# A hybrid attention and DeltaNet layer on one core: the modulation sums of the first stage regrouped, and the attention join moved from VectorE to ScalarE

## The chip, the cores and the metric

The kernel runs on one core of one Trainium2 chip. The core has TensorE (PE in the rows; PEld is its weight load), VectorE (DVE), ScalarE (ACT), GpSimd (POOL) and SyncE (SP), which here only issues loads and stores. The metric is the device time of one launch in microseconds. All tensors are float32; products use fp32r parts.

## The reference

One layer: a modulation vector from the conditioning vector, a wide projection, windowed attention beside a gated DeltaNet, an output projection, and an MLP. What the change touches is the start and the end of the attention:

```
mod = silu(c) @ w_ada + b_ada                 # (1024) @ (1024, 6144)
sh1, sc1, gt1, sh2, sc2, gt2 = split(mod, 6)
u = x * (1.0 + sc1) + sh1                     # (1024, 1024)
proj = u @ w_in                               # q, k, v, DeltaNet inputs, gates
...
o = einsum(probs, v)                          # 16 heads of 64, window of 128
```

## The kernel before

The first stage makes `u`, feature-major, in eight blocks of 128 features. For block `k`, TensorE transposes eight tiles of `x` (`u_turn`, step `t`) into one PSUM bank `b` and one bank `a`; ScalarE reads each bank twice with scale `sc1[:, k]` and bias `sh1[:, k]` (`u_out`, step `o`), once rounded to fp32r (`uh`) and once exact (`utm`); VectorE subtracts the two into the low part `ul`. Then 12 products of 512 columns use the block (`u_mm`, step `m`): two heads of DeltaNet keys, two halves, three products for the split operands.

Before that the block's 128 shifts and 128 scales must exist. Each is a dot product of `silu(c)` with a column of `w_ada`, 8 partial products of 128 rows. They are split by engine: for blocks 2 to 7 the shift is summed by GpSimd (`ada_pool`: a product over 128x1024 and three adds), the scale by VectorE for rows 0 to 5 (`ada_acc`, step `v`: one TENSOR_SCALAR and five SCALAR_TENSOR_TENSOR of 128 columns) and by TensorE for rows 6 and 7 (products of one column with `c_col`, step `p`). TensorE sums the 128 partitions of each partial result with a product against `ones` (step `s`), and VectorE adds the bias into `sc1` and `sh1` (`ada_end`). In block 0 VectorE sums the shift and TensorE the scale; in block 1 GpSimd the shift and TensorE the scale.

The order in which TensorE, VectorE and ScalarE get this work is written by hand, as a string of steps, and the three engines run it in that order. SyncE issues the loads in one queue (`a0 x a1 x d a2 x a3 x ...`: `a` is a block of `w_ada`, two loads of 512 KB; `x` a block of x, 512 KB; `d` two blocks of `w_in`). A load waits when its buffer is still in use: GpSimd, VectorE and TensorE all hold buffers of `w_ada`.

After the first stage come the value projection and the key heads (`pa`), then the attention: 64 items of two heads by 128 queries, threaded between 26 units of 48 products that make queries, keys and gates. Every 16 products one item is started; `after(n, f)` records `f` n products later. The item's last step is `att_values`: four products of 256 columns into the only buffer of PSUM tag `c`. Its two halves of 64 partitions hold two partial sums that must be added. `top` copies the lower half to SBUF (`bot`, ScalarE, five products later) and `join` adds it to the upper half, read from PSUM, in two VectorE operations of 64x128 (four products after that). The bank `c` is free for the next item when the second of these ends. VectorE has long operations in its queue at that time: the triangular solve (`stt`, `M`), weight splits (`wl`), and query splits (`qs`). GpSimd adds the two window halves of the probabilities there (`sm`) and masks them (`pl`).

Of the kernel before, what the change touches and what calls it, by code (L numbers as in the profile page):

```python
# [17 lines left out]
P = 128  # L18
# [16 lines left out]
def hybrid_layer_kernel(ctx: ExitStack, tc: tile.TileContext,  # L35
# [261 lines left out]
    BLK = [(j * P, P) for j in range(KT)]  # L297
    adav, adaa, adat = {}, {}, {}

    ALL = range(KT)  # L300
# [11 lines left out]
    def ada_load(blk):  # L312
        lo, n = BLK[blk]
        m = 2 if n == 256 else 1
        kk = KT // m
        for i in range(m):
            for sec in (0, 1):
                t = ada_tile([P, kk, n])
                nc.sync.dma_start(out=t, in_=w_ada[i * kk * P:(i + 1) * kk * P, sec * D + lo:sec * D + lo + n]
                                  .rearrange("(k p) c -> p k c", p=P))  # L320
                adat[sec, blk, i] = t
                adav.setdefault((sec, blk), []).extend(t[:, k, :] for k in range(kk))

    def ada_acc(sec, blk, ks=range(KT)):
        n = BLK[blk][1]
        if ks[0] == 0:
            adaa[sec, blk, V] = p0.tile([P, n], F32, tag="adaacc1" if sec else "adaaccv", name="adaacc", bufs=1 + sec)
        acc = adaa[sec, blk, V]
        for k in ks:
            w = adav[sec, blk][k]  # L330
            if k == 0:
                V.tensor_scalar(out=acc, in0=w, scalar1=c_col[:, 0:1], scalar2=None, op0=ALU.mult)
            else:
                V.scalar_tensor_tensor(out=acc, in0=w, scalar=c_col[:, k:k + 1], in1=acc, op0=ALU.mult, op1=ALU.add)

    def ada_pool(sec, blk):

# [10 lines left out]
    adap = {}

    def ada_sums(blk, direct):  # L350

        m = BLK[blk][1] // P
        if blk not in adap:
            adap[blk] = psum("a", 2)
        t = adap[blk]
        for sec in (0, 1):
            for j in range(m):
                js = slice(j * P, (j + 1) * P)
                for i, (E, ks) in enumerate(ada_on[sec, blk]):
                    o = 4 * i + 2 * sec + j  # L360
                    if E is T and direct:
                        for k in ks:
                            T.matmul(t[:, o:o + 1], lhsT=adav[sec, blk][k][:, js], rhs=c_col[:, k:k + 1],
                                     start=k == ks[0], stop=k == ks[-1])
                    elif E is not T and not direct:
                        T.matmul(t[:, o:o + 1], lhsT=adaa[sec, blk, E][:, js], rhs=ones[:, 0:1], start=True, stop=True)

    def ada_end(blk):
        lo, n = BLK[blk]
        j0, m = lo // P, n // P  # L370
        t = adap[blk]
        if len(ada_on[1, blk]) > 1:
            V.tensor_tensor(out=sc1[:, j0:j0 + m], in0=t[:, 6:6 + m], in1=bada[:, KT + j0:KT + j0 + m], op=ALU.add)
        V.scalar_tensor_tensor(out=sc1[:, j0:j0 + m], in0=t[:, 2:2 + m], scalar=1.0,
                               in1=sc1[:, j0:j0 + m] if len(ada_on[1, blk]) > 1 else bada[:, KT + j0:KT + j0 + m],
                               op0=ALU.add, op1=ALU.add)
        sh = sh1[:, j0:j0 + m]
        V.tensor_tensor(out=sh, in0=t[:, 0:m], in1=bada[:, j0:j0 + m], op=ALU.add)
        if len(ada_on[0, blk]) > 1:
            V.tensor_tensor(out=sh, in0=t[:, 4:4 + m], in1=sh, op=ALU.add)  # L380
# [11 lines left out]
    rows_a = p0.tile([P, 2 * P], F32, tag="adaacc1", name="rows_a", bufs=2)[:, 0:P]  # L392
# [31 lines left out]
    def u_mm(k):  # L424
        for half in range(2):
            for i in range(2):
                wh, wl = wdk[i]
                for m in range(3):
                    w, xx = ((wh, uh), (wh, ul), (wl, uh))[m]
                    T.matmul(raw_acc[i][half], lhsT=w[:, k, :], rhs=xx[k][:, halves[half]], start=k == 0 and m == 0,  # L430
                             stop=k == KT - 1 and m == 2)

# [1574 lines left out]
```

## Time and profile before

| | |
|---|---|
| Time, median of 3 runs | 1866.16 us (1865.82 to 1868.0) |
| Time of the profiled execution | 1864.97 us |
| Its span, first to last instruction | 1863.3 us |
| TensorE busy | 1820.0 us (98%) |
| VectorE, ScalarE, GpSimd busy | 1306.0, 976.9, 338.5 us |
| Mean granted TensorE clock, of full speed | 0.993 |

The profiled execution has 1.7 us around its span. TensorE is busy for all but 43 us of it, so what shortens the kernel is work taken from TensorE, or one of the stretches in which it waits or runs at the lower clock.

### The profile page before, as it was taken

Reading aid. Unit: us, or ns where it says so; the run is one execution under the profiler, and the core shown is the slowest. Engines: PE = TensorE matmul, PEld = TensorE weight load, DVE = VectorE, ACT = ScalarE, POOL = GpSimd, SP = SyncE. Lnnn points to the kernel's source line nnn. Section 1 sums busy time; section 2 is a strip of 40 time slices with the busy share of each in tenths; the row PEclk is TensorE's granted clock in tenths of the full one; section 3 lists DMA queues with packets and bytes.
Section 4 is the critical chain, followed back from the end, with each engine's and each line's share of the span. In section 5 each row is a group of like instructions: output and inputs, shape, how many; then the busy total and the mean of one; then the engine's idle time right before and its main releaser. Section 6 shows DMA issues by size and latency. Waiting matters only on the chain.

```text
span 1863.3 us, 26105 instructions
## 1 busy us (share of the span) xinstructions
PE 1820.0 (98%) x9161; PEld 1503.1 (81%) x9161; DVE 1306.0 (70%) x2473; ACT 976.9 (52%) x2105; POOL 338.5 (18%) x493
## 2 busy tenths in 40 slices
PE   7999999999999999999999999999999999999997
PEld 5977878878788788888878888877788888888886
DVE  7677688898875566666553445788867776576697
ACT  3789656666664454455553323466555555434441
POOL 7323323443332000000001100002212120000000
PEclk8999999999999999999999999999999999999999
DMA  9655642232248444554355644358887879755671
GB/s 260 178 181 199 216 106 73 84 98 71 69 161 245 131 134 134 160 149 147 111 161 179 212 147 157 116 163 306 301 294 258 264 248 392 279 187 181 196 256 46
DMA packets 262414, 337.74 MB, mean 181 GB/s; under 512 B 26005, under 2 KB 171110, under 8 KB 262026
## 3 DMA queue, kind: packets, MB, share of 16 engines
q1 hardware_dynamic: 222954, 212.94, 36.5%
q0 software_dynamic: 31328, 108.44, 17.3%
q10 hardware_dynamic: 8000, 14.68, 2.2%
q8 instruction: 72, 1.18, 0.3%
q14 instruction: 60, 0.49, 0.1%
HBM read 231.40 MB, written 102.51 MB: 179 GB/s over the span
## 4 chain that ended last, share of the span: by engine, by line
PE 77%; DVE 9%; ACT 4%; DMA 3%; issue 2%; POOL 0%; ACTq 0%; SPq 0%; POOLq 0%; DVEq 0%
PE mm L248 32%; PE mm L1870 7%; PE mm L1930 6%; PE b L1930 4%; PE a L1930 4%; PE b L1870 3%; PE a L1870 2%; PE mm L1499 2%; PE c L1930 2%; PE c L909 2%; PE a L1499 1%; DVE wl L216 1%; PE mm L188 1%; PE mm L187 1%; PE mm L186 1%
## 5 line engine op out<-in xcount | busy, mean ns | idle before, releaser
L248 PE MATMUL mm<-uh,wl 128*128 128x512 f32 x800 | 331.3, 414 | 0.0
L248 PE MATMUL mm<-ul,wh 128*128 128x512 f32 x800 | 320.8, 401 | 0.0
L248 PE MATMUL mm<-uh,wh 128*128 128x512 f32 x800 | 317.3, 397 | 0.0
L216 DVE TENSOR_TENSOR sp<-sraw,sp 128x1024 fp32r<-128x1024 f32 x112 | 132.8, 1219 | 76.8 <-ACT sp L215 76.8
L215 ACT ACTIVATE sp<-sraw 128x1024 fp32r<-128x1024 f32 x112 | 112.7, 1053 | 122.5 <-PE b L1930 75.4
L248 PEld LDWEIGHTS mm<-ul,wh 128*128 128x128 f32 x800 | 150.5, 188 | 26.6 <-issue 0.2
L248 PEld LDWEIGHTS mm<-uh,wl 128*128 128x128 f32 x800 | 151.2, 189 | 22.9 <-issue 3.9
L248 PEld LDWEIGHTS mm<-uh,wh 128*128 128x128 f32 x800 | 151.2, 189 | 21.3 <-issue 0.2
L1930 PE MATMUL mm<-sp 128*128 128x512 f32 x528 | 136.9, 390 | 0.6 <-DVE sp L216 0.6
L1930 PEld LDWEIGHTS mm<-sp 128*128 128x128 f32 x528 | 98.5, 188 | 21.5 <-DVE sp L216 1.4
L216 DVE TENSOR_TENSOR wl<-wr,wh 128x1024 fp32r<-128x1024 f32 x81 | 98.6, 1218 | 8.0 <-ACT wh L215 8.0
L215 ACT ACTIVATE wh<-wr 128x1024 fp32r<-128x1024 f32 x81 | 85.1, 1050 | 22.1 <-PE c L1499 13.8
L1930 PE MATMUL a<-sp 128*128 128x512 f32 x336 | 92.6, 389 | 0.0
L1169 ACT ACTIVATE vn<-a,brk 128x128 f32<-128x128 f32 x64 | 23.5, 368 | 108.1 <-PE a L1167 107.1
L1930 PE MATMUL b<-sp 128*128 128x512 f32 (+1 forms) x336 | 80.0, 374 | 0.0
L842 DVE CUSTOM_DVE_ANT_0 nscore<-a,amask,nsink 128x256 f32<-128x256 f32 (+1 forms) x128 | 54.6, 464 | 33.4 <-PE a L835 32.6
L1930 PEld LDWEIGHTS a<-sp 128*128 128x128 f32 x336 | 63.1, 188 | 13.1
L853 POOL TENSOR_TENSOR sm<-sm 128x256 f32<-128x256 f32 x56 | 55.7, 995 | 97.6 <-ACT sm L849 65.0
L1930 PEld LDWEIGHTS b<-sp 128*128 128x128 f32 x336 | 60.5, 188 | 11.2
L216 DVE TENSOR_TENSOR wl<-fraw,wh 128x1024 fp32r<-128x1024 f32 x43 | 52.5, 1222 | 21.9 <-ACT wh L215 21.5
L849 ACT ACTIVATE sm<-nscore,stat 128x257 f32<-128x257 f32 (+1 forms) x128 | 62.1, 488 | 5.3 <-DVE stat L842 4.9
L215 ACT ACTIVATE wh<-fraw 128x1024 fp32r<-128x1024 f32 x43 | 45.0, 1055 | 33.2 <-PE b L1870 16.3
(524 smaller groups left out, 4669.7 us busy)
## 6 DMA issues: line engine op xcount, KB each, us to landing
wr<-in_w_in_dram SPq DMA_DIRECT2D x60, 512.0 KB, 3.6
sraw<-hf_d SPq DMA_DIRECT2D x54, 512.0 KB, 4.4
fraw<-in_w_ff_dram SPq DMA_DIRECT2D x32, 512.0 KB, 5.2
sraw<-wt_d SPq DMA_DIRECT2D x32, 512.0 KB, 4.3
hf_d<-t ACTq DMA_DIRECT2D x48, 256.0 KB, 4.1
wt_d<-wx POOLq DMA_DIRECT2D x48, 256.0 KB, 3.0
sraw<-in_w_ff_dram SPq DMA_DIRECT2D x22, 512.0 KB, 5.4
adaw<-in_w_ada_dram SPq DMA_DIRECT2D x41, 256.0 KB, 2.7
```

The source lines that it names most:

```text
L186: T.matmul(t, lhsT=wh[:, k, :], rhs=xh[k][:, sl], start=k == 0, stop=False)
L215: A.activation(out=hi, in_=src, func=AF.Copy)
L216: after(lag, lambda: V.tensor_tensor(out=lo, in0=src, in1=hi.bitcast(F32), op=ALU.subtract))
L248: T.matmul(ts[half], lhsT=w[:, k, :], rhs=xx[k][:, sl], start=k == 0 and m == 0, stop=k == KT - 1 and m == 2)
L842: V.tensor_tensor_reduce(out=ns[:, i, 1:1 + W], in0=sc[:, i * 2 * P:i * 2 * P + W], in1=amask[:, mo:mo + W], scale=-1.0, scalar=nsink[:, 2 ...
L849: A.activation(out=sm[:, i, 0:1 + W], in_=ns[:, i, 0:1 + W], func=AF.Exp, scale=-1.0, bias=st[:, i:i + 1], accum_out=st[:, 2 + i:3 + i])
L853: G.tensor_tensor(out=sm[:, :, 1 + P:1 + 2 * P], in0=sm[:, :, 1:1 + P], in1=sm[:, :, 1 + P:1 + 2 * P], op=ALU.add)
L909: T.matmul(av[:, 0:256], lhsT=vt[:, b, :], rhs=p_[:, m, :], start=p_ is full and m == 0, stop=p_ is prods[-1][1] and m == 1)
L1169: after(1, lambda: A.activation(out=vn, in_=Wp[:, 0:P], func=AF.Copy, scale=brk[:, n, h:h + 1]))
L1499: T.matmul(pt, lhsT=m[k][:, tok], rhs=w[:, k % 2, :], start=k == 0 and w is wh and m is mh, stop=k == KT - 1 and m is ml)
L1870: T.matmul(pt, lhsT=a[:, k0 + k, :], rhs=b[k], start=begin and k == 0 and x_ == 0, stop=k == 3 and x_ == 2, skip_group_check=True)
L1930: T.matmul(to, lhsT=a[:, f, t * P:(t + 1) * P], rhs=b[:, f, lo:up], start=(begin or own) and s % NS == 0 and f == 0 and x_ == 0, stop=s % ...
```

## The change

Four edits. Block `k` of `w_ada` now lies in tiles with shift and scale side by side, four row groups to a tile (each tile two loads of 256 KB, 32 loads instead of 16). GpSimd has no part in the sums. VectorE sums shift and scale of a block in one chain of operations 256 columns wide: five of the eight row groups in block 0, four in block 1, seven in blocks 2 to 7 (`ADV`); TensorE takes the rest as one-column products that accumulate into the same PSUM columns as the sum over partitions. The step string is new: TensorE's one-column products of block k+1 stand inside block k-1's products (`mid`), and VectorE's chain of block k+1 is spread around block k's steps. Four small constant operations (`trim`, `sel`) move from later code, where they were scheduled automatically, into the string (`c0`). In the attention, ScalarE copies all four 64x128 quarters of the result out of PSUM, and VectorE adds two SBUF tiles in one operation of 128x128.

```diff
-    ada_on = {(0, 0): [(V, ALL)], (1, 0): [(T, ALL)], (0, 1): [(G, ALL)], (1, 1): [(T, ALL)]}
-    for b in range(2, KT):
-        ada_on[0, b], ada_on[1, b] = [(G, ALL)], [(V, range(6)), (T, range(6, 8))]
+    ADV = [5, 4] + [7] * (KT - 2)
+    w_ada2 = w_ada[:, 0:2 * D].rearrange("(k p) (s d) -> p s k d", p=P, s=2)
...
+        for i in range(2):
+            t = ada_tile([P, 2, 4, P])
             for sec in (0, 1):
+                nc.sync.dma_start(out=t[:, sec, :, :], in_=w_ada2[:, sec, 4 * i:4 * i + 4, blk * P:(blk + 1) * P])
...
-    def ada_pool(sec, blk):
...
+    def ada_direct(blk):
+        adap[blk] = t = psum("a", 2)
+        for sec in (0, 1):
+            for k in range(ADV[blk], KT):
+                T.matmul(t[:, sec:sec + 1], lhsT=adav[blk][k][:, sec, :], rhs=c_col[:, k:k + 1],
+                         start=k == ADV[blk] and sec == 0, stop=False)
+    def ada_sums(blk):
+        for sec in (0, 1):
+            T.matmul(adap[blk][:, sec:sec + 1], lhsT=adaa[blk][:, sec, :], rhs=ones[:, 0:1], start=False, stop=sec == 1)
...
-    def u_mm(k):
+    def u_mm(k, mid=None):
         for half in range(2):
             for i in range(2):
+                if mid and (half, i) == (0, 1):
+                    mid()
...
-    for step in ('t0 s0 o00 o01 w0 w1 d4 t1 s1 v203 o10 v235 o11 v256 m0 t2 p2 s2 v304 o20 v346 o21 m1 t3 p3 s3 v404 o30 v446 o31 m2 '
+    steps = 'p0 v05 b0 t0 s0 v12 e0 o00 o01 w0 v14 w1 p1 d4 t1 s1 v22 e1 v24 o10 v26 o11 v27 m02 t2'
+    for k in range(2, 7):
+        steps += f' s{k} v{k + 1}2 e{k} v{k + 1}4 o{k}0 v{k + 1}6 o{k}1 v{k + 1}7 m{k - 1}{k + 1} t{k + 1}'
+    steps = steps.replace('o50', 'r0 o50').replace('t7', 't7 s7 e7 o70 o71 c0 m6')
...
-        def top():
-            A.activation(out=bot, in_=av[64:128, 0:256], func=AF.Copy)
-            after(4, join)
+        def copy():
+            for i in range(2):
+                for k, dst in ((1, bot), (0, o[:, sl])):
+                    A.activation(out=dst[64 * i:64 * i + 64, :], in_=av[64 * k:64 * k + 64, i * P:(i + 1) * P], func=AF.Copy)
+            after(5, join)
 
         def join():
-                V.tensor_tensor(out=o[64 * i:64 * i + 64, (n % 2) * P:(n % 2 + 1) * P],
-                                in0=av[0:64, i * P:(i + 1) * P], in1=bot[:, i * P:(i + 1) * P], op=ALU.add)
+            V.tensor_tensor(out=o[:, sl], in0=o[:, sl], in1=bot, op=ALU.add)
...
-        after(5, top)
+        after(5, copy)
```

VectorE's queue around block 2's scale and shift, before. `adaacc` is a partial sum, `ul1` the low part of block 1, `a_395` the PSUM columns of block 2's sums:

```order
L332 TENSOR_SCALAR adaacc_358<-adaw_185,c_col_113 128x128
L334 SCALAR_TENSOR_TENSOR adaacc_358<-adaw_185,c_col_113,adaacc_358 128x128 x2
L422 TENSOR_TENSOR ul1_131<-utm_362,uh1_123 128x512
L334 SCALAR_TENSOR_TENSOR adaacc_358<-adaw_185,c_col_113,adaacc_358 128x128 x2
L422 TENSOR_TENSOR ul1_131<-utm_368,uh1_123 128x512
L334 SCALAR_TENSOR_TENSOR adaacc_358<-adaw_185,c_col_113,adaacc_358 128x128
L373 TENSOR_TENSOR sc1_121<-a_395,cols_116 128x1
L374 SCALAR_TENSOR_TENSOR sc1_121<-a_395,sc1_121 128x1
L378 TENSOR_TENSOR sh1_120<-a_395,cols_116 128x1
```

The same engine and place in the changed kernel; `a_363` are block 2's columns, `adaacc_342` block 2's chain and `adaacc_387` block 3's:

```order
L380 TENSOR_TENSOR ul1_131<-utm_355,uh1_123 128x512
L324 SCALAR_TENSOR_TENSOR adaacc_342<-adaw_190,c_col_113,adaacc_342 128x256
L322 TENSOR_SCALAR adaacc_387<-adaw_195,c_col_113 128x256
L324 SCALAR_TENSOR_TENSOR adaacc_387<-adaw_195,c_col_113,adaacc_387 128x256
L342 TENSOR_TENSOR sc1_121<-a_363,cols_116 128x1
L342 TENSOR_TENSOR sh1_120<-a_363,cols_116 128x1
L324 SCALAR_TENSOR_TENSOR adaacc_387<-adaw_195,c_col_113,adaacc_387 128x256 x2
L380 TENSOR_TENSOR ul2_132<-utm_394,uh2_124 128x512
L324 SCALAR_TENSOR_TENSOR adaacc_387<-adaw_198,c_col_113,adaacc_387 128x256
L324 SCALAR_TENSOR_TENSOR adaacc_387<-adaw_198,c_col_113,adaacc_387 128x256
L380 TENSOR_TENSOR ul2_132<-utm_400,uh2_124 128x512
L324 SCALAR_TENSOR_TENSOR adaacc_387<-adaw_198,c_col_113,adaacc_387 128x256
```

Two operations of the next block's chain now stand ahead of a block's `sc1` and `sh1`, and the rest of it between the two `ul`.

TensorE's queue in block 1's products before (`uh1`, `ul1` are the block, `a_440` the columns of block 3):

```order
L413 MATMUL a_386<-ident_89,xin_187 128x128 x4
L363 MATMUL a_395<-c_col_113,adaw_185 128x1 x2
L366 MATMUL a_395<-ones_94,adaacc_236 128x1
L366 MATMUL a_395<-ones_94,adaacc_358 128x1
L430 MATMUL mm_263<-uh1_123,wh_179 128x512
L430 MATMUL mm_263<-ul1_131,wh_179 128x512
L430 MATMUL mm_263<-uh1_123,wl_180 128x512
L430 MATMUL mm_265<-uh1_123,wh_181 128x512
```

And now, where `a_408` are the columns of block 3:

```order
L371 MATMUL a_376<-ident_89,xin_193 128x128 x4
L337 MATMUL a_363<-ones_94,adaacc_342 128x1 x2
L390 MATMUL mm_235<-uh1_123,wh_183 128x512
L390 MATMUL mm_235<-ul1_131,wh_183 128x512
L390 MATMUL mm_235<-uh1_123,wl_184 128x512
L331 MATMUL a_408<-c_col_113,adaw_198 128x1 x2
L390 MATMUL mm_237<-uh1_123,wh_185 128x512
```

The one-column products of block 3 have moved from behind the transposes of block 3 to the fourth place of block 1's products, so TensorE meets them about one block earlier.

ScalarE's queue at one attention item before, `c_2542` being the bank of the values:

```order
L883 ACTIVATE ph_2534<-b_2531 128x256
L914 ACTIVATE bot_2545<-c_2542 64x256
L861 ACTIVATE sm_2495<-sm_2495,stat_2496 128x128 x2
L849 ACTIVATE sm_2550,stat_2551<-nscore0_2090,stat_2551 128x257 x2
L215 ACTIVATE wh_2578<-wr_2387 128x1024
```

And now, `c_2526` being that bank:

```order
L853 ACTIVATE ph_2518<-b_2515 128x256
L890 ACTIVATE bot_2530<-c_2526 64x128
L890 ACTIVATE at_2529<-c_2526 64x128
L890 ACTIVATE bot_2530<-c_2526 64x128
L890 ACTIVATE at_2529<-c_2526 64x128
L831 ACTIVATE sm_2479<-sm_2479,stat_2480 128x128 x2
```

Three more operations stand ahead of the scaling of a later item's probabilities (`sm`), and no VectorE operation reads the bank any more.

## Rows read from the trace of the kernel before

**Rows 1.** Busy time of each engine by stretch (us from the span's start; then the stretch's length, busy us and number of instructions of each engine, granted TensorE clock as a share of full speed, DMA share, GB/s); four stretches of the first stage and one of the attention.

```profile
10.00:20.00 10.00, 9.76 (x53) 8.05 (x54) 6.98 (x12) 4.68 (x6) 5.07 (x5) 0.67 1.12 323
20.00:30.00 10.00, 5.96 (x27) 4.85 (x27) 9.42 (x11) 2.79 (x4) 9.61 (x7) 0.84 1.18 319
30.00:40.00 10.00, 9.18 (x41) 7.42 (x42) 9.23 (x15) 3.36 (x5) 9.42 (x8) 0.84 1.08 287
40.00:50.00 10.00, 5.75 (x26) 4.65 (x25) 9.42 (x17) 4.62 (x8) 6.72 (x7) 0.67 0.66 173
...
300.00:350.00 50.00, 48.20 (x256) 40.30 (x255) 43.18 (x105) 32.98 (x95) 21.41 (x25) 1.00 0.25 81
```

**Rows 2.** What TensorE waited for over the whole span: the instruction that waited, who released it, us in total, times, longest.

```profile
PE a L366 <- DVE adaacc L334: 7.5, 3, 3.5
PE c L909 <- DVE at L922: 6.4, 10, 1.5
```

**Rows 3.** TensorE in order of time in the first stage (start us, us, engine, line, operation, tiles; in brackets the idle time before it and who ended it). L430 is a product of a block, L366 the sum over partitions, L532 the first product of the value projection.

```profile
34.31 0.39 PE L430 MATMUL c<-uh,wl 128*128 128x512 f32 x1
...
36.99 0.48 PE L430 MATMUL mm<-uh,wh 128*128 128x512 f32 x1
...
46.45 0.59 PE L366 MATMUL a<-ones,adaacc 128*128 128x1 f32 x2 [3.36 <-DVE adaacc L334]
...
47.48 0.63 PE L430 MATMUL mm<-ul,wh 128*128 128x512 f32 x1
...
53.00 0.48 PE L430 MATMUL mm<-uh,wh 128*128 128x512 f32 x1
...
57.68 0.48 PE L430 MATMUL mm<-uh,wh 128*128 128x512 f32 x1
...
67.96 0.50 PE L532 MATMUL b<-wvh,uh 128*128 128x272 f32 x2
```

**Rows 4.** VectorE in order of time in the first stage. L334 is the chain of partial sums, L373 and L374 the first operation on a block's scale, L422 a block's low part, L126 the low part of weights.

```profile
18.60 2.36 DVE L126 TENSOR_TENSOR wl<-wr,wh 128x1024 fp32r<-128x1024 f32 x2 [0.18 <-ACT wh L125]
20.88 0.15 DVE L374 SCALAR_TENSOR_TENSOR sc<-a,cols 128x1 f32<-128x1 f32 x1
...
31.21 3.63 DVE L334 SCALAR_TENSOR_TENSOR adaacc<-adaw,c_col,adaacc 128x128 f32<-128x128 f32 x3
...
47.27 0.16 DVE L374 SCALAR_TENSOR_TENSOR sc<-a,sc 128x1 f32<-128x1 f32 x1
...
47.73 1.12 DVE L334 SCALAR_TENSOR_TENSOR adaacc<-adaw,c_col,adaacc 128x128 f32<-128x128 f32 x3
49.07 0.69 DVE L422 TENSOR_TENSOR ul<-utm,uh 128x512 fp32r<-128x512 f32 x1 [0.22 <-ACT utm L421]
49.68 0.73 DVE L334 SCALAR_TENSOR_TENSOR adaacc<-adaw,c_col,adaacc 128x128 f32<-128x128 f32 x2
...
62.38 0.16 DVE L373 TENSOR_TENSOR sc<-a,cols 128x1 f32<-128x1 f32 x1 [0.45 <-PE a L366]
...
66.86 2.36 DVE L126 TENSOR_TENSOR wvl<-wr,wvh 128x1024 fp32r<-128x1024 f32 x2 [0.24 <-ACT wvh L125]
```

**Rows 5.** GpSimd in order of time in the first stage: the product of a block's shift, and the last add of a later block's.

```profile
31.27 2.05 POOL L341 TENSOR_TENSOR adaw<-adaw,c_col 128x1024 f32<-128x1024 f32 x1 [0.19 <-DVE adaacc L332]
...
46.33 0.98 POOL L346 TENSOR_TENSOR adaacc<-adaw 128x128 f32<-128x128 f32 x1
```

**Rows 6.** ScalarE in order of time in the first stage: the rounding of the two key weights, and a block's first exact pass.

```profile
17.50 2.01 ACT L125 ACTIVATE wh<-wr 128x1024 fp32r<-128x1024 f32 x2
...
48.27 0.77 ACT L421 ACTIVATE utm<-b,sh,sc 128x512 f32<-128x512 f32 x1
```

**Rows 7.** Groups of VectorE instructions by shape, whole span (line, operation, tiles, shapes, count, busy us, mean ns of one, idle before).

```profile
L1025 DVE SCALAR_TENSOR_TENSOR ada<-adaw,c_col,ada 128x512 f32<-128x512 f32 x39 | 29.1, 745 | 2.9 <-DMA adaw<-in_w_ada_dram 2.9
...
L1131 DVE SCALAR_TENSOR_TENSOR E<-b,rk,E 128x128 f32<-128x128 f32 x64 | 19.0, 345 | 10.3 <-PE b L1127 10.3
...
L602 DVE CAST gT<-zer 64x1024 fp32r<-64x1024 f32 x1 | 0.8, 764 | 0.1
```

**Rows 8.** Groups by shape in the attention (240 to 580 us), of ScalarE, VectorE and GpSimd: the copy out of PSUM, the join, a product over two SBUF tiles, and the add of the window halves.

```profile
L914 ACT ACTIVATE bot<-c 64x256 f32<-64x256 f32 x64 | 24.5, 382 | 5.4 <-issue 2.7 <-PE c L909 1.3
...
L922 DVE TENSOR_TENSOR at<-c,bot 64x128 f32<-64x128 f32 x128 | 35.6, 278 | 6.6 <-ACT bot L914 5.7
...
L732 DVE TENSOR_TENSOR stt<-M 128x122 f32<-128x122 f32 x1 | 0.3, 286 | 0.0
...
L853 POOL TENSOR_TENSOR sm<-sm 128x256 f32<-128x256 f32 x56 | 55.7, 995 | 97.6 <-ACT sm L849 65.0 <-issue 28.0 <-PE b L877 4.3
```

**Rows 9.** Two places of the attention in order of time, of three engines: L861 scales an item's probabilities, L877 transposes them on TensorE, L909 are the products with the values, L914 and L922 copy and join.

```profile
296.61 0.70 ACT L861 ACTIVATE sm<-sm,stat 128x128 f32<-128x128 f32 x2 [1.82 <-DVE stat L856]
...
335.10 0.38 ACT L914 ACTIVATE bot<-c 64x256 f32<-64x256 f32 x1
335.38 0.69 ACT L861 ACTIVATE sm<-sm,stat 128x128 f32<-128x128 f32 x2
...
336.92 0.38 PE L877 MATMUL b<-ident,sm 128*128 128x128 f32 x2
...
338.53 0.57 DVE L922 TENSOR_TENSOR at<-c,bot 64x128 f32<-64x128 f32 x2
...
339.24 0.47 PE L909 MATMUL c<-ph,vhl 128*128 128x256 f32 x2 [1.47 <-DVE at L922]
```

More of the change, by code (lines that the diff above doesn't have):

```diff
@@ L294, in dummies @@
             T.matmul(warm, lhsT=wz[:, 0:P], rhs=wz, start=True, stop=True)
[L297 to L303 removed]
+    ADV = [5, 4] + [7] * (KT - 2)
+    adav, adaa, adap = {}, {}, {}
+    w_ada2 = w_ada[:, 0:2 * D].rearrange("(k p) (s d) -> p s k d", p=P, s=2)
     aslot = ["gate", "gate", "ks", "wh", "wl", "wh", "wl"] + ["gate", "gate", "ks", "adaw", "adaw"] * 4
@@ L312, in ada_load, with ada_acc @@
     def ada_load(blk):
[L313 to L316, printed above, removed]
+        for i in range(2):
+            t = ada_tile([P, 2, 4, P])
             for sec in (0, 1):
[L318 to L325, printed above, removed]
+                nc.sync.dma_start(out=t[:, sec, :, :], in_=w_ada2[:, sec, 4 * i:4 * i + 4, blk * P:(blk + 1) * P])
+            adav.setdefault(blk, []).extend(t[:, :, k, :] for k in range(4))
+    def ada_acc(blk, ks):
         if ks[0] == 0:
-            adaa[sec, blk, V] = p0.tile([P, n], F32, tag="adaacc1" if sec else "adaaccv", name="adaacc", bufs=1 + sec)
-        acc = adaa[sec, blk, V]
+            adaa[blk] = p0.tile([P, 2, P], F32, tag="adaacc", name="adaacc", bufs=2)
+        acc = adaa[blk]
         for k in ks:
-            w = adav[sec, blk][k]
+            w = adav[blk][k]
             if k == 0:
@@ L348, in hybrid_layer_kernel @@
[L348 to L354, printed above, removed]
-        t = adap[blk]
[L356 to L366, printed above, removed]
@@ L382, in hybrid_layer_kernel, with ada_end @@
+    def ada_sums(blk):
+        for sec in (0, 1):
+            T.matmul(adap[blk][:, sec:sec + 1], lhsT=adaa[blk][:, sec, :], rhs=ones[:, 0:1], start=False, stop=sec == 1)
+    def ada_end(blk):
+        t = adap[blk]
+        for sec, o in ((1, sc1), (0, sh1)):
+            V.tensor_tensor(out=o[:, blk:blk + 1], in0=t[:, sec:sec + 1], in1=bada[:, KT * sec + blk:KT * sec + blk + 1], op=ALU.add)
     xts = []
@@ L431, in u_mm, with sel_make @@
                              stop=k == KT - 1 and m == 2)
+    sel = pv.tile([64, 8, P], F32R, name="sel")
+    selc = pv.tile([64, 8], F32, name="selc")
+    def sel_make():
+        V.tensor_copy(out=trim, in_=tri)
+        V.tensor_scalar(out=trim[0:64, :], in0=tri[0:64, :], scalar1=-1.0, scalar2=None, op0=ALU.add)
+        V.tensor_tensor(out=selc, in0=ident[0:64, 0:8], in1=ident[0:64, 32:40], op=ALU.add)
+        V.tensor_copy(out=sel, in_=bc(selc[:, :, None], [64, 8, P]))
     wvs = []
@@ L482, in hybrid_layer_kernel @@
             tps[k] = u_turn(k)
+        elif f == "b":
+            row_turn(rows_a, cols, "b")
+            V.tensor_scalar(out=bada[:, KT:2 * KT], in0=bada[:, KT:2 * KT], scalar1=1.0, scalar2=None, op0=ALU.add)
         elif f == "s":
-            if k not in direct:
-                ada_sums(k, True)
-            if k:
-                ada_sums(k, False)
+            ada_sums(k)
+        elif f == "e":
             ada_end(k)
         elif f == "p":
-            ada_sums(k, True)
-            direct.add(k)
+            ada_direct(k)
         elif f == "o":
@@ L494, in hybrid_layer_kernel @@
         elif f == "m":
-            u_mm(k)
+            u_mm(k, (lambda b: lambda: ada_direct(b))(int(step[2])) if len(step) > 2 else None)
         elif f == "v":
-            ada_acc(1, k, range(int(step[2]), int(step[3])))
+            to = min(int(step[2]), ADV[k])
+            if to > vdone[k]:
+                ada_acc(k, range(vdone[k], to))
+                vdone[k] = to
         elif f == "d":
-            dummies(int(step[1:]), psum("b", 2))
+            dummies(k, psum("b", 2))
         elif f == "w":
             dk_split(k)
+        elif f == "c":
+            sel_make()
         else:
@@ L505, in hybrid_layer_kernel @@
             A.activation(out=nsink, in_=nsink, func=AF.Copy, scale=-1.0)
+    assert vdone == ADV
     wv_split()
```

56 lines of the change are left out of this document (11 added, 45 removed).

## The prediction

> **What bounds the kernel now.** I first read the busy time by stretch [rows 1], to see where TensorE stops. From 10 to 50 us it is busy 30.65 of 40 us, so 9.3 us are idle, and its clock is granted at 0.67 to 0.84 of full speed; in the attention it is idle 1.8 us in fifty. Next the list of TensorE's waits [rows 2], to see whose fault that is: 7.5 us in the first stage end when VectorE's chain of partial sums is done, and 6.4 us in the attention end when VectorE's join has freed the bank `c`. Third, the engines in order of time. TensorE's longest stop, 3.36 us, ends at 46.45, and the products after it take 0.63 us each (the 1.2 GHz level) where those at 2.4 GHz take 0.39 [rows 3]: a stop costs twice. VectorE shows why the chain is late [rows 4]: three operations of it took 3.63 us at 31.21, while GpSimd was at its share of the next sum from 31.27 on, and the same three took 1.12 us at 47.73, when GpSimd had just finished, at 47.31 [rows 5]. So the first stage is held by VectorE's chain, and the chain is slowed by GpSimd. Six blocks, from the scale of block 1 at 20.88 to that of block 7 at 62.38, took 41.5 us, 6.9 each.
>
> **The first stage, part by part.** The numbers are made against the profiled execution, 1864.97 us; the median of the runs is 1866.16, 1.2 us more, and is what I forecast.
>
> GpSimd's work goes, and with it the slow chain. The new chain operation is 256 wide, which no row shows. It lies between 345 ns at 128 columns and 745 at 512 [rows 7]; on the line between them it is 0.48 us. In a chain each waits for the one before: three of 128 in 1.12 us are 0.37 each, 0.03 over the duration, so I take 0.51. The bounds are 0.37 (the pace at 128) and 0.75. Seven are 3.57 us per block.
>
> VectorE's period for a block is then the chain of the next block, 3.57; two low parts at 0.61 (49.07 to 49.68 [rows 4]), 1.22; the scale and shift, two operations of 0.15 that overlap, 0.2; and one wait. The first low part needs ScalarE's first exact pass, which ends at 49.04 [rows 6], 1.77 us after the block's scale began at 47.27; in that time VectorE has 0.2 plus two chain operations, 1.2 in all, so it waits 0.5. Sum 5.5 us.
>
> TensorE needs less. Full blocks follow each other in 4.68 us (53.00 to 57.68 [rows 3]), and the number of its instructions per block stays as it was. The loads need about as much: a block is 1.05 MB of `w_ada` and 0.52 of `x`, which at 287 to 323 GB/s [rows 1] is 4.9 to 5.5 us; they ran far ahead and fell to 173 GB/s from 40 us on, when buffers were not free. GpSimd no longer holds buffers, so I count no wait for loads; if they set the pace, it is the same 5.5. Splitting a load in two pieces of 256 KB is costed at nothing as long as several are in flight.
>
> New waits: VectorE meets two operations of block k+1's chain before block k's scale, so block k now needs part of the next block's load. TensorE's one-column products of block k+1 wait, in the middle of block k-1's products, for that load and for the bank that block k's scale frees. Behind them stand nine products and the next transposes. With the period of 5.5 all of these are ready in time; in blocks 0 and 1 they are not hidden. There VectorE has the two weight splits (18.60 to 20.96 [rows 4], after ScalarE's rounding at 17.50 [rows 6], which depends on loads that come no earlier) and now two chain operations between them and two behind, 2.0 us, before block 1's scale. Some 0.5 us of this come back, because block 0 is earlier without the small constants ahead of its scale. Block 1's scale moves from 20.88 to about 22.4: 1.5 us lost.
>
> Block 7's scale then comes at 22.4 + 6 x 5.5 = 55.4, against 62.38: 7.0 us gained. From there to the value projection it was 5.6 us (67.96 [rows 3]) and the same products remain. But the four constants now stand ahead of the split of the value weights, whose first half ended at 68.1, at the last moment [rows 4]. The largest, a cast of 64x1024, has a twin of 0.76 us [rows 7]; with the three small ones I take 1.2, of which 1.0 shows. Bounds: 0 and 3. **First stage: 6.0 us gained.** The chain's bounds move the period between 4.7 (TensorE's own) and 7.1, and the gain between 10.8 and a loss of 3.6.
>
> Between 34.70 and 36.99 there were 2.3 us without a product, and the clock stayed up: the next took 0.48 and not 0.63 [rows 3]. In the new order the gap between two blocks' products is 5.5 less 2.85, that is 2.65 us, filled with transposes as that one was. I take the clock as full after block 2.
>
> **The attention join.** All ten stops of TensorE for the join have one form [rows 9]: at 336.92 the transposes are through, two products later the values could start, but the bank is free only when the join ends at 339.10. ScalarE had copied its half by 335.48. Four copies of 64x128 replace the one of 64x256, at 382 ns [rows 8]: each costs between half of that and all of it, 0.28 in the middle, so four are 1.1 us (bounds 0.76 and 1.5), and the bank would be free at 336.2. That lies ahead of every one of the ten, also with 1.5. So 6.4 us are taken away.
>
> On the other side ScalarE gets 0.7 us more in each of 64 items, 45 us in some 310. It is busy 33 of 50 us there [rows 1], and would be 40. What TensorE next needs from it is the scaling of the probabilities, which now stands behind three more copies. At 336.07 that was done 0.85 us before its transposes. The tightest items have 0.2, as at 296.61, but there ScalarE had just waited 1.82 us for VectorE [rows 9], time in which the copies fit. I count 1.0 us of new stops. **Attention: 5.4 us gained**, between 6.4 and a loss.
>
> VectorE's two joins of 278 ns become one of about 286, as a 128x122 product of two SBUF tiles took [rows 8]: 0.27 us less per item, off the path. The join before read PSUM for one operand and took the same time 128 times; now both are in SBUF while GpSimd is busy 21.41 of 50 us with instructions of up to 1 us. The Trainium skill, "SBUF — State Buffer", section "SBUF: two separate sides", says that VectorE with two SBUF inputs and a GpSimd operation that reads SBUF exclude each other for the whole instruction. By that rule a join meets GpSimd in 4 of 10 cases and waits half of 995 ns, 0.2 us, which eats most of those 0.27; by the row of 286 ns alone it does not. Neither enters the sum, since nothing on TensorE waits for the join any more.
>
> **Sum.** 6.0 + 5.4 = 11.4 us: 1853.6 for the profiled execution, 1854.8 for the median. Later stages move as a whole: VectorE, ScalarE and the load queue keep their order after the first stage, apart from the join.
>
> **The rivals.** (1) ScalarE becomes the bound of the attention. For it: 40 of 50 us with every copy ahead of something TensorE needs. It decides when ScalarE's backlog exceeds the 0.85 us or so between scaling and transposes in most items; then up to 0.7 us per item reach TensorE, 45 us less the 6.4: 1866.2 - 6.0 + 38.6 = 1899; half of it is 1880. Against it: ScalarE still waits for TensorE in most items. Slower, 6%. (2) The join frees TensorE only to stop at VectorE's next late result, since VectorE's queue is little shorter. Then only the first stage counts: 1860. 17%. (3) The clock falls in the longer gaps. Products then cost 0.24 more, 2.9 us per block; TensorE's 4.68 becomes 7.6 and holds the period: six blocks take 45.4 and not 33, the first stage loses 6.4, the whole 1867. Against it is the gap of 2.3 us. 9%, no change. (4) The period is nearer to TensorE's 4.7, because the wide operations cost less than the line says: 1850. 13%. (5) The change as costed, 1851.5 to 1858: 55%.
>
> **How the numbers follow.** I forecast 1854.8, the likeliest case; its own range is 1851.5 to 1858. The range reaches to 1849 for (4) and to 1862 for (2), and leaves out (1), (3) and the ends of (4). A measurement of this kernel tells 0.2%, 3.7 us, from no change: (2), (4) and (5) are faster, 0.84 with a little of (2) falling within; (3) is the same, with that rest 0.10; (1) is slower, 0.06.
>
> **What would show it.** In the changed profile: chain operations of 256 at 0.45 to 0.55 us and no 1.2; the scale of block 1 at 22 to 23 and of block 7 near 55; the value projection from about 62; the full clock from 30 us on; no wait for the join at the values; ScalarE near 40 of 50 us at 300. The prediction is wrong if the chain operations stay slow without GpSimd, if TensorE's one-column products wait in the middle of a block, or if a new wait for ScalarE appears at the transposes.

## The result, and the profile after

The changed kernel takes **1856.04 us** (median of 6 runs, 1853.18 to 1860.9) against 1868.08 for the kernel before, measured beside it. One of the six runs before took 2971.85 us and is left out of the ratio, which is **0.9941** (95%: 0.9929 to 0.9953): by it some 11 us less, where the medians differ by 12. The forecast was 1854.8, in a range of 1849 to 1862. The profiled execution has a span of 1853.9 us, 9.4 less than before's.

The time came out near the forecast, but not by the terms of its sum. This table follows one thing: when TensorE starts the same product in both traces (us from the span's start, profiled executions).

| place | before | after | ahead by |
|---|---|---|---|
| first product of the value projection | 67.96 | 62.90 | 5.06 |
| first product on the gates `g` | 103.52 | 100.89 | 2.63 |
| first scores of the attention | 236.85 | 236.71 | 0.14 |
| values of the item at 504.72 before | 504.72 | 495.40 | 9.32 |

The second and third rows of the table, on TensorE before and then after:

```profile
103.52 0.43 PE L581 MATMUL a<-g,tri 128*128 128x64 f32 x2 [0.22 <-DVE g L577]
...
236.85 0.30 PE L834 MATMUL a<-khh,qs 128*128 128x128 f32 x1 [1.51 <-issue]
```

```profile
100.89 0.41 PE L555 MATMUL a<-g,tri 128*128 128x64 f32 x2 [2.01 <-DVE g L551]
...
236.71 0.30 PE L804 MATMUL a<-khh,qs 128*128 128x128 f32 x1 [2.39 <-DMA M<-md_d]
```

The first stage gained 5.06 us where 6.0 were forecast, all but 0.14 of it was given back before the attention began, and the attention gained 9.2 us where 5.4 were forecast.

The busy time by stretch (stretch, length, then busy us and instructions of TensorE, its weight loads, VectorE, ScalarE and GpSimd, granted clock, DMA share, GB/s), to be read against [rows 1]:

```profile
10.00:20.00 10.00, 8.91 (x37) 7.26 (x36) 2.22 (x7) 2.93 (x5) 0.00 (x0) 0.52 1.15 329
20.00:30.00 10.00, 7.49 (x25) 5.58 (x25) 8.91 (x18) 4.65 (x6) 0.00 (x0) 0.67 1.18 320
30.00:40.00 10.00, 9.68 (x57) 8.34 (x56) 6.78 (x19) 5.52 (x8) 0.00 (x0) 0.96 1.06 279
40.00:50.00 10.00, 9.40 (x57) 7.84 (x55) 8.77 (x24) 6.96 (x12) 0.00 (x0) 1.00 1.14 295
99.00:102.00 3.00, 1.11 (x8) 1.04 (x8) 1.51 (x7) 1.24 (x2) 0.00 (x0) 1.00 0.99 372
102.00:105.00 3.00, 3.00 (x16) 2.31 (x16) 2.50 (x6) 1.43 (x7) 0.00 (x0) 0.58 0.05 15
105.00:108.00 3.00, 3.00 (x18) 1.98 (x18) 1.97 (x2) 2.43 (x12) 0.00 (x0) 0.85 0.63 172
300.00:350.00 50.00, 50.00 (x268) 42.10 (x267) 43.18 (x100) 42.11 (x132) 20.80 (x24) 1.00 0.25 81
```

GpSimd is out of the first stage; from 30 us on TensorE is busy 9.4 to 9.7 of 10 at nearly full clock; in the attention it has no idle time left. New are the three short stretches: at 99 to 102 us TensorE works 1.11 of 3 us, and then at 0.58 and 0.85 of its clock, a mean of time at 1.2 and at 2.4 GHz. Before, it was at work and at full clock there:

```profile
99.00:102.00 3.00, 3.00 (x14) 2.46 (x14) 2.59 (x13) 0.08 (x1) 0.93 (x2) 1.00 0.03 9
102.00:105.00 3.00, 2.78 (x17) 2.06 (x16) 1.49 (x8) 1.54 (x2) 0.18 (x1) 1.00 0.90 327
105.00:108.00 3.00, 3.00 (x26) 2.21 (x24) 2.86 (x7) 2.65 (x12) 0.00 (x0) 1.00 0.56 182
```

The list of TensorE's waits after the change names the place:

```profile
PE a L337 <- DVE adaacc L324: 3.7, 6, 2.2
PE a L804 <- DMA M<-md_d: 2.4, 1, 2.4
PE a L555 <- DVE g L551: 2.0, 1, 2.0
```

The 6.4 us for the join [rows 2] are gone, and the 7.5 for the chain are 3.7; 2.0 us for `g` (before: 0.2) and 2.4 at the first scores, put down to the load of M (before: 1.5, put down to issue), stand there now. `g` is made of the raw gates `ba`, which come with the value projection. Why `g` is late is in ScalarE's order of time:

```profile
19.19 0.78 ACT L379 ACTIVATE utm<-a,sh,sc 128x512 f32<-128x512 f32 x1 [3.18 <-PE b L294]
...
91.21 0.42 ACT L515 ACTIVATE vs<-vd 128x256 fp32r<-128x256 f32 x1 [3.10 <-DMA v_d<-vs]
91.54 0.17 ACT L530 ACTIVATE ba<-mm 128x16 f32<-128x16 f32 x1
91.72 1.28 ACT L535 ACT_TABLE_LOAD   x1
```

At 91.21 ScalarE's copy of the last value tile had waited 3.10 us for a store of `v_d`: `vs` has three buffers, and the store that held this one had not landed. Before, the same copy found its buffer free and waited for its input alone:

```profile
93.85 0.42 ACT L539 ACTIVATE vs<-vd 128x256 fp32r<-128x256 f32 x1 [0.93 <-DVE vd L546]
```

Behind it on ScalarE stand, after the change, the raw gates `ba` (91.54) and the gate functions, and on them VectorE's chain to `g`. The other row, at 19.19, is a wait in block 0 that the prediction did not have either.

VectorE in the first stage (L342 is the first operation on a block's scale, L324 the chain):

```profile
24.93 0.15 DVE L342 TENSOR_TENSOR sc<-a,cols 128x1 f32<-128x1 f32 x1
...
42.06 0.15 DVE L342 TENSOR_TENSOR sc<-a,cols 128x1 f32<-128x1 f32 x1
...
43.85 0.69 DVE L380 TENSOR_TENSOR ul<-utm,uh 128x512 fp32r<-128x512 f32 x1 [0.66 <-ACT utm L379]
44.46 1.00 DVE L324 SCALAR_TENSOR_TENSOR adaacc<-adaw,c_col,adaacc 128x256 f32<-128x256 f32 x2
...
47.16 0.15 DVE L342 TENSOR_TENSOR sc<-a,cols 128x1 f32<-128x1 f32 x1
...
57.37 0.16 DVE L342 TENSOR_TENSOR sc<-a,cols 128x1 f32<-128x1 f32 x1 [0.70 <-PE a L337]
```

A block takes 5.10 us (42.06 to 47.16). In the attention, by shape, VectorE's join and one half of ScalarE's copies:

```profile
L894 DVE TENSOR_TENSOR at<-at,bot 128x128 f32<-128x128 f32 x64 | 22.6, 352 | 7.2 <-ACT at L890 7.1
L890 ACT ACTIVATE bot<-c 64x128 f32<-64x128 f32 x128 | 35.1, 274 | 5.3 <-PE c L879 3.2
```

### The profile page after: what moved, and what is told of

Read it like the earlier page. It is cut to its first block, busy times and chain, and to the rows that moved or that the text cites. A ratio compares the mean times of both kernels' runs of the same rounds, so it can differ in the third digit from the quotient of the medians.

```text
span 1853.9 us, 26172 instructions
## 1 busy us (share of the span) xinstructions
PE 1819.3 (98%) x9161; PEld 1504.5 (81%) x9161; DVE 1280.6 (69%) x2411; ACT 1023.1 (55%) x2297; POOL 318.3 (17%) x465
## 4 chain that ended last, share of the span: by engine, by line
PE 81%; DVE 5%; ACT 4%; DMA 4%; issue 2%; POOL 1%; SPq 0%; ACTq 0%; POOLq 0%; DVEq 0%
PE mm L248 35%; PE mm L1841 7%; PE mm L1901 6%; PE b L1901 4%; PE a L1901 4%; PE b L1841 3%; PE a L1841 2%; PE mm L1470 2%; PE c L1901 2%; PE c L879 1%; PE a L1470 1%; PE mm L188 1%; PE mm L187 1%; PE mm L186 1%; DMA sraw<-in_w_ff_dram 1%
## 5 line engine op out<-in xcount | busy, mean ns | idle before, releaser
L864 POOL TENSOR_SCALAR_AFFINE_SELECT pl<-ph 128x512 fp32r<-128x512 f32 x56 | 64.8, 1157 | 74.6 <-DVE ph L857 61.4
L823 POOL TENSOR_TENSOR sm<-sm 128x256 f32<-128x256 f32 x56 | 50.2, 897 | 94.0 <-ACT sm L819 51.8
```

The lines of the kernel that those rows point to most:

```text
L823: G.tensor_tensor(out=sm[:, :, 1 + P:1 + 2 * P], in0=sm[:, :, 1:1 + P], in1=sm[:, :, 1 + P:1 + 2 * P], op=ALU.add)
L864: G.affine_select(out=flat4(part), in_=flat4(full), pattern=[[0, 4], [1 if odd else -1, P]], compare_op=ALU.is_ge if odd else ALU.is_gt, f ...
```

## The experiments

Ratios are to the kernel before, run on the same chip, with 95% intervals; one per cent is 18.7 us.

**1 and 2. Each half alone.** The first: the changed kernel with the old `top` and `join`. The second: the kernel before with the new copies and join.

> The new first stage with the old join of the attention. Theory A (the first stage's gain is given back between the value projection and the first scores of the attention): block 7's scale again near 57.4 us and the value projection near 63, then the stop for `g` near 100 us (2.0 us) with the clock below full behind it, first scores of the attention near 236.7 us as in the kernel before (236.85), and then the old stops for the join: time within 1.5 us of the kernel before. Theory B (the prediction: later stages move as a whole): 5 to 6 us less than the kernel before.

> The old first stage with the new copies and join. Theory A (the join is worth 9.5 us, because a stop of TensorE costs more than the idle time that the trace shows for it): 9 to 10 us less than the kernel before, first scores near 236.9, no stop at the values. Theory B (the prediction's 5.4, 6.4 of recorded stops less 1.0 of new ones): 5 to 6.5 us less.

Measured: first stage alone 1867.87 us, ratio **0.9999 (0.9988 to 1.001)**, no gain. Join alone 1860.42, ratio **0.9961 (0.9947 to 0.9975)**, 4.7 to 9.9 us less. Some of TensorE's waits with the first stage alone:

```profile
PE c L879 <- DVE at L892: 6.2, 9, 1.5
...
PE a L804 <- DMA M<-md_d: 2.5, 1, 2.5
PE a L555 <- DVE g L551: 2.4, 1, 2.4
```

The old stops for the join are there (9 of the 10, 6.2 us), and so are the two new ones. The value projection was 4 us ahead, the product on `g` 1.7, the first scores 0.9 us behind (237.75), and behind this stop the clock was granted at 0.70 from 238 to 242 us. So the prediction's 6.0 us did not reach the end. With the join alone TensorE was 2.5 us late at 242.6 (M landed later in that execution, with the same drop of the clock) and 6.8 us ahead at the values of 504.72: 9.3 us in the attention, as in the changed kernel; 1.2 of them are lost at 571 to 591, where E and the queries are late. The time of the join alone fits both of its theories (9 to 10 us, 5 to 6.5); the 9.3 us are of one trace. The two ratios add up to 7.5 us, the changed kernel has 11; with intervals of 2 to 3 us each this doesn't tell an interaction from none.

**3 and 5. The gates ahead of the store's wait, by order.**

```
# 3: ba copied ahead of keep(vd, t) and keep(vraw, ...)
+                A.activation(out=ba[:, t, :], in_=pt[:, 256:272], func=AF.Copy)
                 if t:
                     keep(vd, t)
...
# 5: the same, and the last tile's keep behind the gate functions
+                if 0 < t < NT - 1:
+                    keep(vd, t)
...
             A.activation(out=y, in_=y, func=AF.Exp, scale=-1.0)
+            keep(vd, NT - 1)
```

> The changed kernel with the copy of the raw gates (`ba`) on ScalarE moved ahead of the two `keep` copies, which wait for a store buffer of `vs`. Theory A1 (what is given back is the stop for `g` and the lower clock behind it): `g` is ready some 2.5 to 3 us earlier, no stop at L555 near 98.5 us, full clock from 100 to 110 us, and 2 to 3.5 us less than the changed kernel (1852.5 to 1854). Theory A2 (M's landing at 235.9 us holds TensorE at the first scores, whatever comes before it): the stop at L555 goes too, but the one at the first scores grows by as much from its 2.4 us: no difference in time over 0.5 us.

> The changed kernel with the copy of the raw gates (`ba`) ahead of the `keep` copies, and the last tile's `keep` behind ScalarE's three gate operations (in the run before this, the gate operations still stood behind the last `vs` copy and its wait). Theory A1: VectorE's `g` (L551) is done 2 to 3 us earlier, near 97.5 us; no stop over 0.5 us at the first product on `g`; the clock full from 102 to 108 us, where the changed kernel has 0.58 and 0.85; the first scores come 2.5 to 3.5 us earlier, at 233 to 234.5, and the time is 2 to 3.5 us less than the changed kernel's. Theory A2: the stop at the first scores grows by what is gained: the same time within 1 us.

Measured: 1856.0 us, ratio 0.9937 (0.9922 to 0.9952), and 1859.27, ratio 0.9955 (0.9939 to 0.9970): neither differs from the changed kernel. Both edits missed their aim. In the third the stop at `g` was still 1.42 us, in the fifth 2.42: `ba` was copied early (89.17 and 88.85), but the scheduler left the last `vs` ahead of ScalarE's gate functions in both, and they waited with it (2.36 us, to 91.39, in the fifth). The cause was not taken away, so neither says anything on it. Both traces show a later stop instead, 3.4 and 3.6 us for T near 575 us; the profiled execution was the slowest of its six in both.

**4. The buffer of the dummy products.**

```
-    wz = p0.tile([P, HALF], BF16, tag="utm", name="wz", bufs=2)
+    wz = p0.tile([P, HALF], BF16, name="wz")
```

> The changed kernel with a buffer of its own for `wz`, the zeros that TensorE's dummy products read, which shares the two buffers of `utm`. Theory A (ScalarE's fourth pass of block 0 waits 3.18 us for the dummy products, since they read the buffer that it must write): that wait goes, block 1's scale comes near 22.5 us instead of 24.93 and the value projection near 60.5 instead of 62.9; whether the time follows by 2 us or not at all is told by the first scores near 236.7. Theory B (the wait is for the transposes or the one-column products on TensorE): block 1's scale stays within 0.5 us of 24.9.

Measured: **1850.36 us, ratio 0.9906 (0.9888 to 0.9924)**, 6.5 us less than the changed kernel. ScalarE's fourth pass of block 0 and VectorE's scales of blocks 1, 2 and 7:

```profile
15.96 0.78 ACT L379 ACTIVATE utm<-a,sh,sc 128x512 f32<-128x512 f32 x1
```

```profile
22.07 0.15 DVE L342 TENSOR_TENSOR sc<-a,cols 128x1 f32<-128x1 f32 x1
27.17 0.15 DVE L342 TENSOR_TENSOR sc<-a,cols 128x1 f32<-128x1 f32 x1
...
53.09 0.16 DVE L342 TENSOR_TENSOR sc<-a,cols 128x1 f32<-128x1 f32 x1 [0.70 <-PE a L337]
```

The pass ran at 15.96 instead of 19.19, block 1's scale came 2.86 us earlier, block 2's 4.67 (from 31.84; the stop of 2.2 us ahead of block 1's sums went, too, and with it the 1.2 GHz, a granted clock of 0.50, from 24 to 30 us), block 7's 4.28. So the wait was for the dummy products, which read the buffer that the pass must write. These 4.3 us lay ahead of the hand-over at `g`; there TensorE stopped for 1.75 us, but the clock stayed at 1.00 this time. The gain was more than the 2 us expected: in the traces this kernel is 4.3 us ahead of the changed one at the value projection, 5.9 behind the stop at `g`, and 5.0 at 700 us.

**6. M's load on another queue.**

```
-    nc.gpsimd.dma_start(out=Mf, in_=md_d...)
+    nc.sync.dma_start(out=Mf, in_=md_d...)
```

> The changed kernel with the 2 MB load of M issued on SP's queue instead of GpSimd's, ahead of the copies of `khh` and `kll`. Theory A (TensorE's 2.4 us at the first scores are the wait for `khh`'s other half, whose copy stands behind M in one queue): the stop falls below 0.5 us, the first scores begin near 234.4 instead of 236.7, and the time is 1.5 to 2.5 us less than the changed kernel's. Theory B (the DMA engines are full, whichever queue the copy stands in: their share is 1.4 there): the stop stays over 1.5 us and the time does not move.

Measured: 1856.6 us, ratio 0.9940 (0.9923 to 0.9956), the same as the changed kernel. In the trace the stop at the first scores is gone (none over 0.3 us), and they begin at 233.38; so what TensorE waited for there was the copy of `khh` behind M in one queue. But 1.8 us for T and 0.6 for E came at 572 and 582, and the time shows nothing of it.

**7. GpSimd at work beside the new chain.**

```
+    for _ in range(32):
+        G.tensor_tensor(out=gs, in0=gs, in1=gs, op=ALU.add)      # 128x512
```

> The changed kernel with 32 additions of 128x512 on GpSimd during the first stage, on a buffer that nothing else reads. The prediction's reason (VectorE's chain was slow because GpSimd was at work): the chain's operations at 256 columns, 0.48 us without GpSimd, go to 1 us or more while GpSimd works, a block takes 7 to 10 us instead of 5.1, and the value projection begins 8 us or more later than 62.9. Rival (the chain was slow for another reason, such as the operands' layout): 0.48 to 0.55 us and 5.1 us per block.

Measured, in a single run: 1874.94 us. VectorE while GpSimd works, and after 44.9 us, when it has ended:

```profile
30.61 2.30 DVE L324 SCALAR_TENSOR_TENSOR adaacc<-adaw,c_col,adaacc 128x256 f32<-128x256 f32 x2
32.83 1.52 DVE L380 TENSOR_TENSOR ul<-utm,uh 128x512 fp32r<-128x512 f32 x1
...
48.88 0.99 DVE L324 SCALAR_TENSOR_TENSOR adaacc<-adaw,c_col,adaacc 128x256 f32<-128x256 f32 x2
50.53 0.69 DVE L380 TENSOR_TENSOR ul<-utm,uh 128x512 fp32r<-128x512 f32 x1 [0.66 <-ACT utm L379]
```

A chain operation takes 1.15 to 1.25 us beside GpSimd and 0.48 without, a block 11.1 us (30.47 to 41.55) and 5.1; the value projection came 12 us later. This is the rule of the Trainium skill, "SBUF — State Buffer", section "SBUF: two separate sides" (VectorE with two SBUF inputs and a GpSimd operation that reads SBUF exclude each other for a whole instruction). By that rule, the trace agrees: GpSimd's additions took 1.165 us each on average, and where VectorE's chain operations follow each other beside them they start 1.15 to 1.29 us apart, about one to an addition.

**8. ScalarE's slack in the attention.**

```
+            for i in range(2):
+                A.activation(out=bot2[64 * i:64 * i + 64, :], in_=av[0:64, 0:P], func=AF.Copy)
```

> The changed kernel with two more copies of 64x128 on ScalarE behind the four in each of the 64 items of the attention, into a buffer that nothing reads: ScalarE goes from 42 to about 46.5 of 50 us. Theory A (ScalarE has slack up to a full queue): no stop of TensorE over 0.3 us in the attention, and within 2 us of the changed kernel. Rival (the prediction's case 1: each copy stands ahead of something that TensorE needs): stops at the transposes (L847) or the values, up to 0.54 us per item, 10 to 35 us slower.

Measured: 1858.37 us, ratio 0.9951 (0.9935 to 0.9968). ScalarE is busy 46.1 of 50 us at 300, and TensorE has new stops at the transposes:

```profile
PE b L847 <- ACT sm L831: 2.1, 7, 0.8
```

The attention gains 4.1 us over before where the four copies alone gain 9.2, so two more cost 5.1. Neither theory holds: there is slack at 42 of 50 us and not enough at 46, and the cost is far from the 10 us or more of the rival. Something else shows earlier in this trace. Up to the attention this kernel has the changed kernel's instructions, but in its execution the store had landed in time: ScalarE's last `vs` waited for its input alone (0.93 us, at 88.54), there was no stop at `g`, the clock stayed full, and the first scores began at 232.24.

**9 and 10. A buffer for the last store.** The last tile's `vs` takes the buffer of `kd`, which has no use yet; the ninth on the changed kernel, the tenth on the first stage alone (experiment 1).

```
+                    if b == NT - 1:
+                        vs = pa.tile([P, S], F32, tag="kd", name="kd", bufs=1)[:, 0:4 * P]...
```

> The changed kernel with the last tile's `vs` in a buffer of its own (that of `kd`, not used yet), so that ScalarE's copy into it cannot wait for an earlier store of `v_d`. In the trace of the run with two more copies, whose instructions are the same up to the attention, that wait happened not to come, and there was no stop at `g` and the first scores began at 232.2 us. Theory A1 (that wait is what gives the first stage's gain back): L551's `g` done near 98 us, no stop over 0.3 us at L555, the clock full from 99 to 108 us, first scores at 231.5 to 233.5, and the time 2 to 4 us less than the changed kernel's. Theory A2 (a later hand-over takes it back): first scores still near 236 or a longer stop for T near 575 us, and the same time within 1 us.

> The new first stage with the old join, as in the first experiment, and with the last tile's `vs` in its own buffer. Theory A1: the gain of the first stage, 4 to 5 us at the value projection, now arrives at the first scores (232 to 233.5 against 236.85) and in the time: 3.5 to 5 us less than the kernel before, where the first experiment had none. Theory A2: no gain again.

Measured: 1852.03 us, ratio 0.9921 (0.9907 to 0.9935); and on the first stage alone 1861.25, ratio **0.9969 (0.9959 to 0.9980)**, where it was 0.9999 (0.9988 to 1.001) without the buffer. ScalarE in the ninth:

```profile
88.76 0.42 ACT L518 ACTIVATE kd<-vd 128x256 fp32r<-128x256 f32 x1 [0.93 <-DVE vd L525]
89.08 0.17 ACT L533 ACTIVATE ba<-mm 128x16 f32<-128x16 f32 x1
89.27 1.28 ACT L538 ACT_TABLE_LOAD   x1
```

Everything is 2.4 us earlier than at 91.21, no stop at `g` is left, the clock is 1.00 from 99 to 108 us, and the first scores begin at 232.44 in the ninth and 232.49 in the tenth. The intervals of the first and the tenth run lie apart: with one buffer more the new first stage is worth 3.7 to 7.7 us. The buffer on the kernel before was not run; in that kernel's trace the copy waits for no store, so there was nothing for it to take away in that execution. The interval of the ninth overlaps the changed kernel's by a hair, with the median 4 us lower.

**11 and 12. Together.** Both buffers; and with M on SP's queue too.

> The changed kernel with own buffers for `wz` and for the last `vs`. If the two add: value projection near 58.5 to 60, no stop at `g`, first scores at 227.5 to 229.5, and 6 to 9 us less than the changed kernel (1847 to 1850). If `wz` alone already gives what there is: the same as the run with `wz` alone within 1 us (6.5 us less than the changed kernel by the ratio to the kernel before).

> The same with M's load on SP's queue too, which took the stop of 2.4 us at the first scores away but left the time as it was. If the later loads (T, E) set the end of the attention: the same as the run with the two buffers within 1.5 us. If they don't: 1.5 to 2.5 us less than that run.

Measured: **1849.12 us, ratio 0.9904 (0.9890 to 0.9918)**, the fastest here, 7 us less than the changed kernel; and 1849.27, ratio 0.9911 (0.9897 to 0.9925). First scores at 228.02 and 225.99. `wz` alone had 0.9906: what the second buffer adds to it is not to be seen, and M's queue adds nothing, since 2.7 us are lost for E at 574 us in that trace.

## Why the prediction was right, and where not

**The cause of the slow chain: right.** 0.48 us per operation, as read off the line between 128 and 512 columns, and experiment 7 puts the slowness back by GpSimd alone. Right behind one another they do start 0.51 us apart, as taken. But most of the seven do not stand behind one another: ahead of other work the next operation starts after 0.40, and the first of a block, a product alone, took 0.35. So the seven take 3.1 us instead of 3.57, and the block 5.1 instead of 5.5. The other terms stood: two low parts 1.21, scale and shift 0.14 (0.2), a wait of 0.66 for ScalarE (0.5).

**Block 1's scale: wrong.** 24.93, not 22.4. The two chain operations between the weight splits and two behind are there as forecast; the step left out that ScalarE's pass needs the buffer that the dummy products read, which now stand behind the one-column products of block 1 (16 instructions in the trace, 3.58 us from 13.85 on). Experiment 4 has 22.07. The stop behind it cost the clock as well: TensorE ran at 1.2 GHz from 24 to 30 us, and block 2's scale waited 1.72 us for it. Block 7's scale came at 57.37 (55.4) and the value projection at 62.9 (62); the four constants cost a stop of 0.37 us there, not 1.0.

**"Later stages move as a whole": wrong**, and the dearest step. The order was kept, as said, but a store's landing does not move with the order. Of 5.06 us, 0.5 went at the split of the value weights, 1.9 at `g`, 1.5 by the lower clock behind that stop, and 1.0 by the first scores. Before, ScalarE's last value copy waited 0.93 us for its input and found its buffer free; the prediction did not look at how near the store was. Experiments 1 and 10 show it by the time: 0 and 5.8 us (3.7 to 7.7; forecast: 6.0).

Why the store was late in some executions was not tried by itself, but the traces sort it. Here are VectorE's split of a key weight and GpSimd's part of the tile whose store holds the buffer, in the changed kernel and then in experiment 8:

```profile
84.74 1.21 DVE L126 TENSOR_TENSOR wl<-wr,wh 128x1024 fp32r<-128x1024 f32 x1
84.84 1.71 POOL L516 TENSOR_TENSOR vs<-vd,vs 128x256 fp32r<-128x256 f32 x1 [1.11 <-DVE kT L610]
```

```profile
84.36 0.74 POOL L516 TENSOR_TENSOR vs<-vd,vs 128x256 fp32r<-128x256 f32 x1 [0.98 <-ACT vs L515]
84.39 1.79 DVE L126 TENSOR_TENSOR wl<-wr,wh 128x1024 fp32r<-128x1024 f32 x1
```

The one that starts first takes its short time, and the other the long one. With GpSimd second, the store is issued 0.08 us behind the copy of `kt_d` (86.58 and 86.50), and ScalarE's copy that waits for it starts 4.6 us later; with GpSimd first, it is issued 0.73 us ahead of that copy (85.13 and 85.86), and it has landed within 3.4 us. All ten traces without an own buffer for the last `vs` fall in these two kinds: in seven GpSimd's part took 1.45 to 1.71 us and ScalarE waited 1.4 to 3.8 us for the store; in three (before, experiments 2 and 8) it took 0.74 to 1.04 us, and ScalarE waited for its input alone. In the ninth it took 1.67, and the buffer made it harmless. Whether the later issue or the copy of `kt_d` ahead makes the store land late is open.

**Attention, 5.4 us forecast, 9.2 found: the mechanism right, the size off.** The stops vanished, a copy took 0.27 us (0.28), ScalarE went to 42 of 50 us (40), and the 1.0 us of new stops did not come. What was mis-sized is the price of a stop, 6.4 us for ten. Here is one, on TensorE before, and then the same products after:

```profile
397.91 0.40 PE L248 MATMUL mm<-ul,wh 128*128 128x512 f32 x1
399.51 0.47 PE L909 MATMUL c<-ph,vhl 128*128 128x256 f32 x2 [1.20 <-DVE at L922]
399.82 0.40 PE L909 MATMUL c<-pl,vhl 128*128 128x256 f32 x2
```

```profile
394.02 0.39 PE L248 MATMUL mm<-ul,wh 128*128 128x512 f32 x1
394.25 0.39 PE L879 MATMUL c<-ph,vhl 128*128 128x256 f32 x2
394.48 0.40 PE L879 MATMUL c<-pl,vhl 128*128 128x256 f32 x2
```

In a stream the next product starts 0.23 us after the last began, though each has a record of 0.39; a stop is counted only from the record's end. So 0.17 us more are lost at its start, and 0.08 behind it (0.31 for 0.23): 1.45 us for a stop of 1.20. Eleven stops (the ten of [rows 2], 6.4 us, and one of 0.4 that the list puts down to issue) at 0.25 more each make 9.6, an estimate from this one stop; 9.2 were found.

**The join beside GpSimd.** The row of 286 ns was right for 54 of 64 joins (median 281); ten took 0.50 to 0.85 us, exactly those that started while GpSimd was computing (two that started beside its issue of a DMA took 0.28), and the mean is 352. By the rule of the Trainium skill's "SBUF — State Buffer", section "SBUF: two separate sides", the prediction had an estimate of 0.2 us for each join, 4 of 10 meeting GpSimd for half of an instruction. It was 0.07: the ten lost 0.46 us each, near that half, but they were 10 of 64. TensorE did not wait for it, as said.

**The rest.** The clock at 0.80 from 30 to 32 us and full from there to the stop at `g`, no one-column product waiting over 0.3 us in mid-block, no stop at the values: as forecast. Rival 1 is real but farther off: it begins past 42 of 50 us and costs 5 us at 46. That the time came out so near was luck. In the profiled execution 0.1 us of the first stage's 6.0 arrived, 5.9 too few, and the attention gave 3.8 too many: 9.3 of 11.4 us, two wrong terms that cancel in part.

## What to carry to other kernels

A gain ahead of a hand-over through memory is not a gain until the copies, stores and buffers there are checked one by one: look for the buffer whose store must land next, and for what stands behind that wait on the same engine. Follow one product through both traces at a handful of places; the end time alone would have hidden that one half gave nothing here. Where two engines start almost together and delay each other, as VectorE and GpSimd do at 84.4 to 84.8 us, the order can differ from one execution to the next, so a buffer that was free in one trace need not be free in the next. Count a stop of TensorE from where the next product would have started, not from the end of the record.

## What the runs showed of the hardware

The clock after a stop was not the same each time. After the stop at `g` it was granted at 0.58 from 102 to 105 us (changed kernel, 2.0 us; experiment 3, 1.42 us) and at 0.62 in experiment 6 (1.74 us), but it stayed at 1.00 in experiment 4 (1.75 us); after the first scores it was 0.70 from 238 to 242 in experiment 1 (2.5 us) and 1.00 in the changed kernel (2.4 us). Here 0.50 would be 1.2 GHz throughout and 1.00 is 2.4 GHz; the values between are means over the stretch. The drop cost 1.5 us at `g`. No run here says what decides it. In experiment 7 operations of VectorE with one SBUF tile and a column of scalars slowed as well (first chain term 1.12 us against 0.35).
